# Expert routing: the lower weight parts of seven "up" chunks move from GpSimd to VectorE

## The chip, the cores and the metric

The kernel runs on one core of a Trainium2 chip. The metric is the device time of the whole program in microseconds (us), from launch to the last output. Engines are named as in the profile: PE (TensorE), DVE (VectorE), ACT (ScalarE), POOL (GpSimd), SP (SyncE, which here issues the weight loads).

## What is computed

Three transformer blocks on 256 tokens of width 1024. The change touches the end of the first block, a product-key expert layer ("PEER"), of which this is the reference, cut:

```python
q = (ht @ w_q).reshape(T, PEER_HEADS, PEER_QDIM)
s1 = einsum('thd,nd->thn', q[..., :128], sub_k1); s2 = einsum('thd,nd->thn', q[..., 128:], sub_k2)
v1, i1 = top_k(s1, 16); v2, i2 = top_k(s2, 16)
cand = v1[..., :, None] + v2[..., None, :]          # 16 x 16 candidates per head
vals, pos = top_k(cand, 16)                          # 16 of 128*128 experts, for each of 8 heads
experts = take_along_axis(cand_idx, pos); gates = softmax(vals)
a = einsum('cd,chkd->chk', x, expert_u[experts])     # "up"
w = gelu(a) * gates
out = einsum('chk,chkd->cd', w, expert_v[experts])   # "down"
```

## The kernel before

It does not gather. It multiplies all 256 tokens with all 16384 expert rows ("up", 64 chunks of 256 experts), applies gelu, and later multiplies with a dense matrix of gates that the routing builds from the selected indices.

**Split weights.** Each float32 weight chunk arrives by one SP-issued DMA into `raw` (three buffers). `stream` then makes two parts of it: ACT writes the upper part `wh` (L99, two halves of 128x1024), and L101 writes the lower part `wl = raw - wh` in two halves, on DVE, or on POOL where `pool` is true. `wh` and `wl` have three buffers each, so ACT can begin chunk c+3 only when PE has done chunk c; the load of chunk c+3 into `raw` is issued when both halves of `wl` of chunk c are made. PE needs three products for each block of 128 (L117 to L119): the first two read `wh`, the third reads `wl`. A chunk is two outputs of 24 matmuls each, half 0 and half 1. Each output lies in one of two PSUM buffers (tag `tq`) until ACT has applied gelu to it (`ga`, L1020).

**Routing.** While PE does the query projection and then the first "up" chunks, DVE does the top-16 searches and the selection, for the token tiles t0 and t1 in turn: the candidates (L923), eight searches by MAX8, FIND_INDEX8, MATCH_REPLACE8 (L891 to L895), the softmax of the gates (`g`, L934 to L939, whose Exp is on ACT at L935 between two table loads), some integer work on positions (L943 to L957), then for each of two index lists a one-hot product (`eq`, L962 to L971: 128x2048 in 16-bit), whose result `idx` PE transposes (L973). After t1 follow 32 groups that build gates as one-hot matrices (E, B, A: L996 to L1000; matmuls L1005).

**Order.** `weave` lets the routing go one step and takes one "up" chunk at steps 7 to 19, so chunks 0 to 12 lie beside the searches and selections of t0 and t1; then two chunks in five steps. A scheduler then sets the order of the instructions on each engine, each of which runs its own in order. It sets DVE's splits where it holds them to be due, and ACT's Exp and PE's transposes of `idx` in between the gelus and the matmuls.

**Names.** Chunks 3 to 6 have the lower parts `wl_3500`, `wl_3575`, `wl_3650`, `wl_3718`; chunks 7 and 8 `wl_3809` and `wl_3895`; chunks 9 to 11 `wl_3992`, `wl_4067`, `wl_4142`; chunk 12, which is on DVE in both kernels, `wl_4210`. The transposed indices are `idx_3567`, `idx_3642` for t0 and `idx_4059`, `idx_4134` for t1. In the profile all of these are `wl` and `idx`.

Of the kernel before, what the change touches and what calls it, by code (L numbers as in the profile page):

```python
# [857 lines left out]
class Peer:  # L858
# [153 lines left out]
    def up(self):  # L1012
        k, nc = self.k, self.k.nc
        for c in range(64):
            hl = k.stream(k.a["peer_u"][c], pool=c < 12)
            for i in range(2):
                ps = k.tp((128, S), tag="tq")
                k.linear_stat(hl, i, ps)
                g = self.pool.tile([128, S], F32, tag="ga", name="ga", bufs=self.AHEAD)
                nc.scalar.activation(g, ps, AF.Gelu_apprx_tanh)  # L1020
                self.ga[c * 2 + i] = g
            yield

    def down(self, up):
        k, nc, pool = self.k, self.k.nc, self.rp
        acc = [[k.acc(name=f"o{t}{h}") for h in range(2)] for t in range(2)]
# [14 lines left out]
        for c in range(64):  # L1041
            if c % 4 == 0:
                G = pool.tile([128, S // self.GRP, 8, self.GRP], F32, tag="g8", name="G", bufs=2)
                nc.scalar.dma_start(G, self.gd[:, :, c * 2:c * 2 + 8, :])
            for _ in range(1 if c else 5):
                next(up, None)
            vs = [x.rearrange("p (e h n) -> p e h n", e=2, h=2) for x in k.stream(k.a["peer_v"][c])]
            ws = []
            for i in range(2):
                e = c * 2 + i  # L1050
                w = self.ga.pop(e)
                w3 = w.rearrange("p (a b) -> p a b", b=self.GRP)
                nc.vector.tensor_tensor(w3, w3, G[:, :, e % 8, :], op=OP.mult)
                wh = pool.tile([128, S], F32R, tag="wth", name="wth", bufs=5)
                wl = pool.tile([128, S], F32R, tag="wtl", name="wtl", bufs=5)
                k.split(wh, wl, w)
                ws.append((wh, wl))
            if c < 62:
                for i in range(2):
                    part(c * 2 + i, vs, ws[i])  # L1060
            else:
                last += [(c * 2 + i, vs, ws[i]) for i in range(2)]
# [11 lines left out]
    def run(self):  # L1074
        up = self.up()
        done = [0]

        def n(i):
            x = i >= 7 if i < 20 else i % 5 in (0, 3)
            x = min(x, self.AHEAD // 2 - 5 - done[0])  # L1080
            done[0] += max(x, 0)
            return max(x, 0)
        with self.k.tc.tile_pool(name="route", bufs=1) as self.rp:
            weave(self.routing(), up, n)
        with ExitStack() as ctx:
            self.rp = ctx.enter_context(self.k.tc.tile_pool(name="down", bufs=1))
            self.k.work(ctx)
            self.down(up)
# [850 lines left out]
```

## Time and profile before

| | |
|---|---|
| median of 3 runs | 2859.41 us (2853.96 to 2859.89) |
| profiled execution | 2853.05 us, of it 2851.1 us span from first to last instruction |
| PE busy | 2744.9 us, 96% of the span |
| DVE busy | 1786.7 us, 63% |
| ACT busy | 1364.5 us, 48% |
| POOL busy | 294.8 us, 10% |

The stretch that the change touches lasts from about 343 us (chunk 3) to about 425 us (chunk 12). Shares over the whole span tell nothing of it; the windows and timelines of that stretch, in the section on rows, do. In a timeline a number in square brackets is the idle time of the engine just before the row, and the name behind it what ended that time.

### The profile page before, as it was taken

The numbers are of one execution on the slowest core, as the hardware profiler recorded it, in microseconds if no ns is written. First come the engines' busy times: TensorE is split into PE (matmuls) and PEld (weight loads), VectorE is DVE, ScalarE is ACT, GpSimd is POOL, SyncE is SP. The second block draws the span as 40 slices with busy tenths as digits, with TensorE's granted clock in tenths as the row PEclk, the third lists the DMA queues.
The fourth block names the chain that finished last, engine by engine and source line by source line (L and its number), as shares of the span: only waits on it lengthen the run. The fifth ranks groups of instructions, "written<-read, shape, count | busy, mean of one in ns | idle before, by whom it ended". The sixth has DMA issues, their size and how long they took to land.

```text
span 2851.1 us, 44585 instructions
## 1 busy us (share of the span) xinstructions
PE 2744.9 (96%) x18132; PEld 2481.8 (87%) x18132; DVE 1786.7 (63%) x3018; ACT 1364.5 (48%) x2302; POOL 294.8 (10%) x314
## 2 busy tenths in 40 slices
PE   7899979999999999999999999999999999999999
PEld 6787979989999888988899899897998878889897
DVE  6757698775555556547865555676645665466654
ACT  5544445544444555444544444524444454454543
POOL 2101650000000000003300000151001110000100
PEclk9989999999999999999999999999999999999999
DMA  5423436896565555554255455524554334433452
GB/s 207 152 97 134 150 121 254 288 321 219 204 215 205 192 192 198 201 190 167 87 188 190 165 209 189 196 89 148 193 192 142 134 116 156 161 133 121 161 192 104
DMA packets 105982, 496.74 MB, mean 174 GB/s; under 512 B 11040, under 2 KB 44320, under 8 KB 50224
## 3 DMA queue, kind: packets, MB, share of 16 engines
q1 hardware_dynamic: 61632, 443.15, 44.8%
q10 hardware_dynamic: 44144, 50.74, 5.4%
q8 instruction: 142, 2.33, 0.3%
q14 instruction: 64, 0.52, 0.1%
HBM read 476.03 MB, written 17.83 MB: 173 GB/s over the span
## 4 chain that ended last, share of the span: by engine, by line
PE 63%; issue 23%; DVE 7%; POOL 3%; ACT 3%; DMA 1%; POOLq 0%; ACTq 0%; DVEq 0%
PE acc L119 6%; PE acc L117 6%; PE acc L118 6%; PE tp L119 4%; PE tp L117 4%; PE tp L118 4%; PE o L1037 4%; PE o L1036 4%; PE o L1039 4%; PE o L316 2%; PE o L317 2%; PE o L319 2%; DVE wl L101 1%; PE o L1667 1%; PE o L1664 1%
## 5 line engine op out<-in xcount | busy, mean ns | idle before, releaser
L101 DVE TENSOR_TENSOR wl<-raw,wh 128x1024 fp32r<-128x1024 f32 x808 | 972.0, 1224 | 633.9 <-ACT wh L99 633.2
L99 ACT CAST wh<-raw 128x1024 fp32r<-128x1024 f32 x848 | 862.4, 1041 | 712.2 <-PE acc L118 234.9
L118 PE MATMUL acc<-xx,wh 128*128 128x256 f32 x1504 | 423.9, 282 | 0.0
L119 PE MATMUL acc<-xx,wl 128*128 128x256 f32 x1504 | 423.4, 281 | 0.0
L117 PE MATMUL acc<-xx,wh 128*128 128x256 f32 x1504 | 423.2, 281 | 0.0
L117 PE MATMUL tp<-xx,wh 128*128 128x256 f32 (+1 forms) x1440 | 410.7, 285 | 5.6 <-ACT ga L1020 5.6
L119 PE MATMUL tp<-xx,wl 128*128 128x256 f32 (+1 forms) x1440 | 409.0, 284 | 2.1 <-DVE wl L101 2.1
L118 PE MATMUL tp<-xx,wh 128*128 128x256 f32 (+1 forms) x1440 | 408.6, 284 | 0.0
L117 PEld LDWEIGHTS acc<-xx,wh 128*128 128x128 f32 x1504 | 284.9, 189 | 0.3 <-ACT xs L278 0.3
L119 PEld LDWEIGHTS acc<-xx,wl 128*128 128x128 f32 x1504 | 285.1, 190 | 0.0
L118 PEld LDWEIGHTS acc<-xx,wh 128*128 128x128 f32 x1504 | 283.0, 188 | 0.0
L117 PEld LDWEIGHTS tp<-xx,wh 128*128 128x128 f32 x1440 | 274.0, 190 | 9.1 <-ACT ga L1020 6.0
L118 PEld LDWEIGHTS tp<-xx,wh 128*128 128x128 f32 x1440 | 274.1, 190 | 2.5
L119 PEld LDWEIGHTS tp<-xx,wl 128*128 128x128 f32 x1440 | 273.5, 190 | 2.5 <-DVE wl L101 2.5
L117 PE MATMUL acc<-wh,xx 128*128 128x256 f32 (+2 forms) x672 | 228.3, 341 | 2.5 <-ACT xx L112 2.2
L118 PE MATMUL acc<-wl,xx 128*128 128x256 f32 (+2 forms) x672 | 223.5, 333 | 5.3 <-DVE wl L101 5.3
L147 POOL TENSOR_SCALAR va<-ss 128x1 f32<-128x1 f32 (+1 forms) x49 | 24.3, 496 | 1949.8 <-ACT junk L143 1768.1
L119 PE MATMUL acc<-wh,xx 128*128 128x256 f32 (+2 forms) x672 | 221.9, 333 | 2.1 <-DVE xx L113 2.1
L1037 PE MATMUL o<-wl,wth 128*128 128x512 f32 x512 | 200.2, 391 | 2.1 <-DVE wl L101 2.1
L1036 PE MATMUL o<-wh,wth 128*128 128x512 f32 x512 | 200.7, 392 | 0.0
L1039 PE MATMUL o<-wh,wtl 128*128 128x512 f32 x512 | 159.6, 390 | 0.0
L118 PEld LDWEIGHTS acc<-wl,xx 128*128 128x128 f32 x672 | 132.2, 197 | 16.7 <-DVE wl L101 6.9
(508 smaller groups left out, 4853.4 us busy)
## 6 DMA issues: line engine op xcount, KB each, us to landing
raw<-in_ffn_in_dram SPq DMA_DIRECT2D x88, 1024.0 KB, 4.9
raw<-in_peer_u_dram SPq DMA_DIRECT2D x64, 1024.0 KB, 5.0
raw<-in_peer_v_dram SPq DMA_DIRECT2D x64, 1024.0 KB, 4.9
raw<-in_ffn_out_dram SPq DMA_DIRECT2D x44, 1024.0 KB, 4.9
raw<-in_w_up_dram SPq DMA_DIRECT2D x32, 1024.0 KB, 4.9
raw<-in_w_down_dram SPq DMA_DIRECT2D x32, 1024.0 KB, 4.9
gd<-gt ACTq DMA_DIRECT2D x16, 1024.0 KB, 5.9
G<-gd ACTq DMA_DIRECT2D x16, 1024.0 KB, 7.0
```

The costliest lines, as they stand in the source:

```text
L99: nc.scalar.copy(h[:, c], r[:, c])
L101: eng.tensor_tensor(l[:, c], r[:, c], h[:, c].bitcast(F32), op=OP.subtract)
L117: mm(out, ah, bh, start=start, stop=False)
L118: mm(out, ah, bl, start=False, stop=False)
L119: mm(out, al, bh, start=False, stop=stop)
L316: mm(acc[t][h], hi[:, k, ts], wv[0][:, h], start=st, stop=False)
L317: mm(acc[t][h], hi[:, k, ts], wv[1][:, h], start=False, stop=False)
L319: mm(acc[t][h], lo[:, k, ts], wv[0][:, h], start=False, stop=sp)
L1036: mm(acc[t][h], wh, vh[:, h], start=st, stop=False)
L1037: mm(acc[t][h], wh, vl[:, h], start=False, stop=False)
L1039: mm(acc[t][h], wl, vh[:, h], start=False, stop=sp)
L1664: mm(acc[t][h], xh, wh[:, h], start=st, stop=False)
```

## The change

The lower parts of chunks 3 to 6 and 9 to 11 are made by DVE; those of 0, 1, 2, 7 and 8 stay on POOL, and from 12 on nothing is different.

```diff
         for c in range(64):
-            hl = k.stream(k.a["peer_u"][c], pool=c < 12)
+            hl = k.stream(k.a["peer_u"][c], pool=c in (0, 1, 2, 7, 8))
```

The scheduler orders the rows anew on DVE, ACT and PE; SP's order stays. On DVE, at the end of t0's searches (`mr`, `val`, `pos` are the search's, `g` is the gates' softmax):

```order
 L895 MAX_INDEX pos_3289<-val_3288,mr_3388 128x8
 L893 MATCH_REPLACE mr_3394<-val_3288,cand_3285 128x112
-L962 CAST ib_3559<-i1_2473 128x128
+L101 TENSOR_TENSOR wl_3500<-raw_3497,wh_3499 128x1024
 L894 MAX val_3288<-mr_3394 128x8
-L962 CAST ib_3634<-i2_2474 128x128
+L101 TENSOR_TENSOR wl_3500<-raw_3497,wh_3499 128x1024
 L895 MAX_INDEX pos_3289<-val_3288,mr_3394 128x8
 L934 TENSOR_TENSOR g_3462<-val_3288 128x128
```

Both halves of chunk 3's split stand behind all eight searches, and ahead of the last search's two final steps and of `g`.

On DVE, from t0's second one-hot product to the second `idx` and the candidates of t1 (`eq_3561` is the first product, `eq_3636` the second), the rows before:

```order
L967 TENSOR_TENSOR eq_3636<-eq_3636,ib_3634 128x2048
L969 TENSOR_TENSOR eq_3561<-eq_3561 128x512
L969 TENSOR_TENSOR eq_3636<-eq_3636 128x1024
L969 TENSOR_TENSOR eq_3561<-eq_3561 128x256
L969 TENSOR_TENSOR eq_3636<-eq_3636 128x512
L971 TENSOR_TENSOR idx_3567<-eq_3561 128x128
L969 TENSOR_TENSOR eq_3636<-eq_3636 128x256
L923 TENSOR_TENSOR cand_3777<-v1_2471,v2_2472 128x8x64
L971 TENSOR_TENSOR idx_3642<-eq_3636 128x128
```

and of the change:

```order
L971 TENSOR_TENSOR idx_3567<-eq_3561 128x128
L967 TENSOR_TENSOR eq_3636<-eq_3636,ib_3634 128x2048
L101 TENSOR_TENSOR wl_3650<-raw_3647,wh_3649 128x1024
L969 TENSOR_TENSOR eq_3636<-eq_3636 128x1024
L101 TENSOR_TENSOR wl_3650<-raw_3647,wh_3649 128x1024
L969 TENSOR_TENSOR eq_3636<-eq_3636 128x512
L101 TENSOR_TENSOR wl_3718<-raw_3715,wh_3717 128x1024
L969 TENSOR_TENSOR eq_3636<-eq_3636 128x256
L101 TENSOR_TENSOR wl_3718<-raw_3715,wh_3717 128x1024
L971 TENSOR_TENSOR idx_3642<-eq_3636 128x128
```

The first `idx` is no longer mixed with the second product, and the splits of chunks 5 and 6 stand between it and the second `idx`; chunk 4's split stands just ahead of these rows, inside the first product's tree (L969).

On ACT, the place of t1's Exp, before:

```order
L99 CAST wh_3894<-raw_3892 128x1024
L935 ACT_TABLE_LOAD
L935 ACTIVATE g_3954<-g_3954 128x128
L1020 ACT_TABLE_LOAD
L1020 ACTIVATE ga_3748<-tp_3723 128x256
```

and of the change:

```order
L1020 ACTIVATE ga_3839<-tp_3814 128x256
L935 ACT_TABLE_LOAD
L935 ACTIVATE g_3954<-g_3954 128x128
L1020 ACT_TABLE_LOAD
L1020 ACTIVATE ga_3866<-tp_3841 128x256
```

`ga_3748` is the gelu of chunk 6's half 0, `ga_3839` and `ga_3866` those of chunk 7's two halves: the Exp stands three gelus later. t0's Exp stays ahead of chunk 3's first gelu, with one cast more in front of it. On PE the first two matmuls of half 1 of chunks 4 and 5 move ahead of half 0's third, and the transpose of the first `idx` stands after 10 matmuls of chunk 4's half 1 instead of 16, that of the second after 17 of chunk 5's half 1 instead of ahead of chunk 5. In t1 ten rows of the one-hot groups (E, B, A, each 128x1024 in 16-bit) that lay ahead of the second `idx` on DVE come behind it, and the first half of chunk 12's split comes ahead of it.

## Rows read from the trace of the kernel before

**Rows 1.** The page, part 1: busy us, share of the span, instructions.

```profile
PE 2744.9 (96%) x18132; PEld 2481.8 (87%) x18132; DVE 1786.7 (63%) x3018; ACT 1364.5 (48%) x2302; POOL 294.8 (10%) x314
```

**Rows 2.** Windows: stretch, length, busy of each engine, granted clock, DMA share, GB/s.

```profile
361.90:378.50 16.60, 6.63 (x41) 6.35 (x41) 16.53 (x30) 5.25 (x8) 7.20 (x3) 0.80 0.37 127
...
392.90:417.30 24.40, 18.85 (x145) 18.59 (x145) 24.40 (x35) 11.14 (x17) 16.82 (x7) 0.93 0.39 131
```

**Rows 3.** Waits of PE, 340 to 424: waiter, releaser, us, times, longest.

```profile
PE tp L973 <- DVE idx L971: 10.1, 3, 7.3
PE tp L117 <- ACT ga L1020: 5.6, 2, 2.9
```

**Rows 4.** Timeline of PE: start, us, engine, line, op, [idle before, releaser].

```profile
356.40 0.28 PE L119 MATMUL tp<-xx,wl 128*128 128x256 f32 x1
356.52 0.28 PE L117 MATMUL tp<-xx,wh 128*128 128x256 f32 x1
...
364.70 0.39 PE L117 MATMUL tp<-xx,wh 128*128 128x256 f32 x1 [2.70 <-ACT ga L1020]
364.92 0.28 PE L118 MATMUL tp<-xx,wh 128*128 128x256 f32 x1
...
368.82 0.28 PE L117 MATMUL tp<-xx,wh 128*128 128x256 f32 x1
...
378.50 0.44 PE L973 MATMUL tp<-ident,idx 128*128 128x128 f32 x1 [7.28 <-DVE idx L971]
...
387.01 0.27 PE L977 MATMUL tp<-ident,g 128*128 128x128 f32 x1
...
395.87 0.58 PE L117 MATMUL tp<-xx,wh 128*128 128x256 f32 x1 [2.92 <-ACT ga L1020]
...
417.30 0.33 PE L973 MATMUL tp<-ident,idx 128*128 128x128 f32 x1 [2.63 <-DVE idx L971]
...
423.46 0.33 PE L973 MATMUL tp<-ident,idx 128*128 128x128 f32 x1 [0.16 <-DVE idx L971]
```

**Rows 5.** Timeline of POOL: chunk 8's split, then those of chunks 10 and 11.

```profile
388.26 4.78 POOL L101 TENSOR_TENSOR wl<-raw,wh 128x1024 fp32r<-128x1024 f32 x2 [1.85 <-ACT wh L99]
...
404.40 11.89 POOL L101 TENSOR_TENSOR wl<-raw,wh 128x1024 fp32r<-128x1024 f32 x4 [2.79 <-ACT wh L99]
```

**Rows 6.** Timeline of DVE, rows that lie beside a split on POOL.

```profile
349.14 2.21 DVE L923 TENSOR_TENSOR cand<-v,v 128x512 f32<-128x512 f32 x1
...
363.33 2.34 DVE L957 TENSOR_TENSOR xb<-x,y 128x128 f16<-128x128 f32 x1
...
388.16 0.26 DVE L893 MATCH_REPLACE8 mr<-val,cand 128x112 f32<-128x112 f32 x1
388.34 2.45 DVE L962 CAST ib<-i 128x128 f16<-128x128 uint32 x1
...
404.76 3.42 DVE L965 TENSOR_TENSOR eq<-xb,iota 128x2048 f16<-128x2048 f16 x1
```

**Rows 7.** Timeline of DVE, rows with POOL idle.

```profile
360.61 0.25 DVE L962 CAST ib<-i 128x128 f16<-128x128 uint32 x1
...
361.41 0.26 DVE L934 TENSOR_TENSOR g<-val 128x128 f32<-128x128 f32 x1
...
373.73 1.22 DVE L965 TENSOR_TENSOR eq<-xb,iota 128x2048 f16<-128x2048 f16 x1
374.86 0.69 DVE L969 TENSOR_TENSOR eq<-eq 128x1024 f16<-128x1024 f16 x1
...
423.33 4.62 DVE L101 TENSOR_TENSOR wl<-raw,wh 128x1024 fp32r<-128x1024 f32 x4
```

**Rows 8.** Timeline of ACT: t1's Exp.

```profile
393.82 0.31 ACT L935 ACTIVATE g<-g 128x128 f32<-128x128 f32 x1 [2.95 <-DVE g L934]
```

**Rows 9.** DMA issues, 330 to 440: queue, op, count, KB each, median us to landing.

```profile
raw<-in_peer_u_dram SPq DMA_DIRECT2D x14, 1024.0 KB, 4.9
```

**Rows 10.** Windows: the one-hot groups behind the change, columns as in rows 2.

```profile
440.00:540.00 100.00, 97.87 (x1033) 95.78 (x1032) 94.45 (x136) 58.96 (x103) 0.00 (x0) 0.98 0.72 262
```

## Prediction

> **What bounds the kernel now.** First the page: PE is busy for 96% of the span [rows 1], so a change elsewhere pays only where PE waits or runs slowly. The windows around chunks 3 to 12 show two such places: from 361.9 to 378.5 PE is busy for 6.6 of 16.6 us, from 392.9 to 417.3 for 18.9 of 24.4, while DVE has no gap in either [rows 2]. The waits of PE there have two releasers: `idx` on DVE (10.1 us) and a gelu on ACT (5.6 us) [rows 3]. The timeline of PE gives the places: 2.70 us at 364.70, 7.28 at 378.50, 2.92 at 395.87, 2.63 at 417.30, 0.16 at 423.46, in all 15.7 us [rows 4]. The waits for a gelu are DVE's too: ACT stood before the Exp, which waited 2.95 us for DVE's `g` [rows 8], and the gelu was queued behind it. So DVE bounds this stretch.
>
> After three of these waits PE also runs slowly: at 364.70 the next matmul starts 0.22 us later, against 0.12 at 356.40, and the granted clock of that window is 0.80 of the 2.4 GHz level, which is what a part at 1.2 GHz gives [rows 2, 4]. The slow spacing ends just before 368.82 [rows 4]: some 18 matmuls of 0.095 us too much, 1.7 us. Three times that is 5.1 us. **The loss before is 15.7 + 5.1 = 20.8 us.**
>
> **Why DVE is late.** Beside a split on POOL many DVE rows take 2.2 to 3.4 us. An L962 takes 2.45 beside POOL and 0.25 with POOL idle; an L965 3.42 and 1.22 [rows 6, 7]. Their ends fit the ends of POOL's halves (a split of two halves lasts 4.78 [rows 5]): each waits for one half, some 2.2 us. MATCH_REPLACE8 beside POOL takes 0.26: the searches don't wait [rows 6]. I count twelve such rows from 349 to 417, 26 us together; five are shown. When both engines have work queued they take turns: at 404.40 POOL's four halves stretch to 11.89 us, 2.97 each [rows 5].
>
> **The change, part by part.** *Removed from POOL:* seven splits. With them the twelve waits of DVE go, if nothing new collides (two of them lie beside chunk 8, which stays on POOL, but those rows now come ahead of it): -26 us on DVE. *Added to DVE:* 14 halves of 1.14 us (four in 4.62 [rows 7]): +16.0 us. *Moved:* ten one-hot rows go behind the second `idx` of t1, 0.6 each by the row of that size [rows 7], -6.1; chunk 12's split comes ahead of it, +2.3 or half of that. ACT and PE get no work added; SP's order is the same.
>
> The total doesn't say where PE waits, so I follow the new order with the durations of these rows.
>
> *Chunk 3.* Its split stands behind eight searches. DVE's row at 349.14 no longer waits, which brings all behind it forward by 1.6 us, so the split starts where L962 stood, 360.61 - 1.6 = 359.0 [rows 6, 7], and its first half is there at 360.2. PE starts this chunk at 356.52 and needs `wl` at the third matmul, 356.75 [rows 4]: **a new wait of 3.5 us**, and by the rows above a slow clock behind it, 1.7. Before, PE did not wait here. Queued behind the split on DVE are `g` and the Exp; `g` comes at 361.7 instead of 361.41 [rows 7], and the gelu that the Exp holds up isn't due until PE ends the half at 364.5, so this wait (2.70 before) is gone. PE ends chunk 3 at 367.4.
>
> *Chunk 4.* From `g` to the second product row DVE needs 5.8 us unhindered (1.9 to L957 [rows 6, 7], 1.4 for eight small rows, 2.5 for the large ones), to 367.5; the first half is there at 368.75, PE has waited 0.4 for a gelu and 0.5 for the split. `idx_3567` is there at 372.65, when PE gets to it: 0.15. **In all 1.1 us, where 7.28 was.**
>
> *Chunks 5 to 7.* DVE goes on with the second product and chunk 5's split, to 376.6; PE waits 0.25 for a gelu. But chunk 7 is still POOL's. Its load goes out when chunk 4's split is done, at 370.4, and takes 4.9 [rows 9]; ACT casts it from 375.5, so POOL starts at 376.5. DVE then has a tree row, chunk 6's two halves, another tree row and `idx_3642` queued, 3.2 us of work of the kind that waits. Taking turns, it waits for both halves of POOL, 4.6 us: `idx_3642` at 384.3 instead of 379.7. PE stands before it from 379.7: **4.7 us, and 1.7 of slow clock.** By this PE ends chunk 6's half 0 at 389.5; before it began at 387.01 [rows 4] and ended 2.8 later, at 389.9. Up to here all is spent again.
>
> On this the Trainium skill, SBUF — State Buffer, section "Who interferes with whom", says that a DVE instruction with two SBUF inputs contends with a GpSimd instruction that reads SBUF, that whichever issues first holds the port for its whole length, and that one with a single SBUF input outside the fast modes doesn't contend. The rows above agree (2.21 and 0.26 us); were DVE to issue first at 376.6, this rule would give the lighter collision, the first rival.
>
> *t1.* PE now needs 2.84 us for each half (24 times 0.118) from 389.5 on. Chunk 8 on POOL runs from 387.4 to 392.2 beside searches, which don't wait. Searches end at 394.6, then chunk 9's split, needed by PE at 403.8: no wait. `g` at 397.5, Exp, table load, gelu at 399.7; since the Exp stands three gelus later, PE doesn't need that buffer before 400.9. **The 2.92 goes, with its slow clock.** Nothing on POOL hinders the products: `idx_4059` at 409.3, PE there at 409.5; `idx_4134` at 414.1 to 414.2, PE there at 415.25. **The 2.63 goes.** The DVE account agrees: 423.3 (the end of that `idx` before, where the splits of [rows 7] begin) - 6.1 + 16.0 + 2.3 - 26 + 4.6 = 414.1.
>
> *Behind it.* From 440 to 540 DVE is busy for 94 of 100 us and PE for 98 [rows 10]. DVE enters it about 7 us earlier than before and PE 8; the 6 us in which DVE is not busy there cover the difference of 1, so I count it as nothing. Without that cover it costs that 1 us.
>
> **Sum.** Loss after: 3.5 + 1.7 + 1.1 + 0.25 + 4.7 + 1.7 = 13.0. Gain 20.8 - 13.0 = 7.8; the walk (415.35 against 423.5 at chunk 11) gives 8.2. I take 8. On the profiled execution, 2851.1 span and 2 around it, that is 2853.05 - 8 = 2845. The median of the three runs is 2859.41, 6.4 above it; taken from the median, which is what will be compared, 2851.4, rounded to **2851**. Bounds: a slow clock may or may not follow a wait (it did not after 2.63 us [rows 4]): 1.7 either way for each of the two, so 4.6 to 11.4 by the clock alone.
>
> **Rivals.**
> *A lighter collision at chunk 7.* If DVE gets through more rows first, or the load of chunk 7 lands later, one half of POOL is waited for, or none. For: the order of two queued engines hangs on tenths of a us. Against: ACT has the cast ready before DVE's queue is through. Price: 2.4 to 4.7 us and the slow clock of 1.7 saved, gain 10.5 to 14.5: 2845 to 2849. Chance 0.18.
>
> *t1 loses again.* The margins there are 0.1, 1.0 and 1.2 us. If two DVE rows of t0's gates (L981, L982) come 0.4 us later, they meet chunk 8's first half, and all of t1 is 2.4 us later; a wait of 1 to 3 us and a slow clock take 3 to 5 back: gain 3 to 5, 2855. Likewise if chunk 3's wait is longer by some us. With all that ends within 0.2% (5.7 us, what a measurement here can tell from no change): 0.24.
>
> *DVE's long rows are not POOL's doing, so the splits only add.* Then `idx_4134` comes at 423.3 - 6.1 + 16.0 + 2.3 = 435.5, 12 us later than before, and PE with it: 2871. It decides from the point where less than 12 of the 26 us are relieved. Against it speak the short rows with POOL idle [rows 7]; for it only that a wait for a port isn't itself a row. Chance 0.06.
>
> That the change does nothing is excluded: the order shows the 14 rows on DVE.
>
> **How the numbers follow.** Forecast (gain 5.7 to 10.5) 0.52, lighter collision 0.18, within 0.2% 0.24, slower 0.06. Faster by over 0.2%: 0.52 + 0.18 = 0.70. The range: from 2842 (10 to 11 us below the profiled execution, since an execution may lie there rather than at the median) to 2858 (a gain of 1.5 from the median).
>
> **What would show it.** Right: one wait of PE for `wl` near 356.8 of about 3.5 us; one for `idx` near 379.7 of about 4.7, beside chunk 7 on POOL; none of over 1 us between 390 and 425; L953, L954, L965 and L967 at their short lengths except beside chunks 7 and 8; `idx_4134` near 414. Wrong: a PE wait for chunk 4, 5, 9 or 10's `wl` of several us, DVE rows still long with POOL idle, or the later one-hot stage growing by what was gained.

## The result, and the profile after

The changed kernel takes 2839.82 us (median of 9 runs, 2833.34 to 2848.18), the kernel before beside it 2857.15 (9 runs): ratio 0.9945, 95% interval 0.9931 to 0.9960. It is faster, by more than forecast (2851), and the time lies below the range (2842 to 2858).

The profiled execution took 2846.34 us, span 2844.6. Page, part 1, of the kernel after:

```profile
PE 2746.9 (97%) x18132; PEld 2483.8 (87%) x18132; DVE 1781.1 (63%) x3032; ACT 1364.4 (48%) x2302; POOL 261.8 (9%) x300
```

VectorE has 14 rows more than in [rows 1] and yet is busy 5.6 us less; GpSimd gave up 33. The waits of TensorE, 340 to 424, that answer to [rows 3]:

```profile
PE tp L119 <- DVE wl L101: 4.1, 2, 3.8
PE tp L117 <- ACT ga L1020: 3.5, 3, 3.0
```

No wait for `idx` is left, where there were 10.1 us. The places, in TensorE's timeline, answer to [rows 4]:

```profile
356.26 0.39 PE L119 MATMUL tp<-xx,wl 128*128 128x256 f32 x1 [3.81 <-DVE wl L101]
...
363.98 0.39 PE L117 MATMUL tp<-xx,wh 128*128 128x256 f32 x1 [0.24 <-ACT ga L1020]
...
388.25 0.58 PE L117 MATMUL tp<-xx,wh 128*128 128x256 f32 x1 [3.00 <-ACT ga L1020]
```

The first is chunk 3's new wait for its split; the last is a wait for a gelu ahead of chunk 7's half 1, where none was forecast (its path is shown under "Which chunks on GpSimd still cost"). The first L910 stands at 295.8 here and at 299.8 in the trace before, so times of the prediction are to be read 4.0 us earlier. Windows after, columns as in [rows 2]:

```profile
343.04:361.90 18.86, 15.05 (x114) 14.84 (x113) 18.86 (x107) 8.60 (x13) 0.00 (x0) 0.91 0.17 58
361.90:378.50 16.60, 15.81 (x130) 15.15 (x129) 16.50 (x26) 7.53 (x14) 5.87 (x1) 1.00 0.38 128
378.50:392.90 14.40, 11.40 (x84) 11.19 (x83) 14.40 (x73) 5.77 (x10) 7.67 (x4) 0.88 0.58 221
392.90:417.30 24.40, 24.40 (x209) 24.40 (x209) 24.40 (x45) 13.47 (x23) 0.00 (x0) 1.00 0.51 183
```

From 361.9 to 378.5 TensorE is now busy for 15.81 of 16.60 us, where it was 6.63. Two stretches with a lowered clock are left (0.91, 0.88), each about a wait; there were three, two of them in [rows 2] (0.80, 0.93) and one between:

```profile
378.50:392.90 14.40, 14.39 (x107) 14.25 (x107) 14.40 (x69) 6.80 (x11) 9.40 (x4) 0.87 0.22 75
```

**A measure with less scatter.** The medians carry the scatter of the whole program: the changed kernel's runs alone lie 15 us apart. I therefore measure in each trace the stretch from the start of the first score matmul (L910, queries times keys) to the start of the last one-hot matmul (L1005). It is 299.8 to 544.1 = 244.3 us before and 295.8 to 529.1 = 233.3 after; copies of both give 244.3 and 233.0 (below). It has two parts. Up to the first L1005 it is 135.2 us before and 125.6 after, in the copies 135.2 and 125.5: **there the change is worth 9.6 to 9.7 us.** The rest, the one-hot groups, takes 109.1 and 107.7 us. This 1.4 is a slow clock of TensorE, which stands behind the same wait before and not after. The wait and the window from it to the end of the groups, before and then after:

```profile
535.28 0.38 PE L119 MATMUL tp<-xx,wl 128*128 128x256 f32 x1 [2.08 <-DVE wl L101]
535.28:544.30 9.02, 9.02 (x85) 8.79 (x86) 3.51 (x4) 4.09 (x7) 0.00 (x0) 0.81 0.65 242
...
521.72 0.39 PE L119 MATMUL tp<-xx,wl 128*128 128x256 f32 x1 [2.08 <-DVE wl L101]
521.72:529.30 7.58, 7.58 (x86) 7.40 (x87) 3.52 (x4) 3.99 (x7) 0.00 (x0) 1.00 0.73 276
```

The copies agree with this, but of the two traces of another kernel (chunks 0 to 2 alone on GpSimd, below) one has this slow clock and one hasn't (109.0 and 107.6). So the whole stretch gains 11.0 to 11.3 us, and whether the 1.4 in it belongs to the change is open.

### The profile page after: what moved, and what is told of

Same layout as the page of the kernel before. It is cut to its first block, busy times and chain, and to the rows that moved or that the text cites. A ratio compares the mean times of both kernels' runs of the same rounds, so it can differ in the third digit from the quotient of the medians.

```text
span 2844.6 us, 44587 instructions
## 1 busy us (share of the span) xinstructions
PE 2746.9 (97%) x18132; PEld 2483.8 (87%) x18132; DVE 1781.1 (63%) x3032; ACT 1364.4 (48%) x2302; POOL 261.8 (9%) x300
## 4 chain that ended last, share of the span: by engine, by line
PE 63%; issue 23%; DVE 6%; POOL 3%; ACT 3%; DMA 3%; ACTq 0%; POOLq 0%; DVEq 0%; SPq 0%
PE acc L119 6%; PE acc L117 6%; PE acc L118 6%; PE tp L119 4%; PE tp L117 4%; PE tp L118 4%; PE o L1037 4%; PE o L1036 4%; PE o L1039 4%; PE o L316 2%; PE o L317 2%; PE o L319 2%; DVE wl L101 2%; PE o L1667 1%; PE o L1665 1%
## 5 line engine op out<-in xcount | busy, mean ns | idle before, releaser
L101 DVE TENSOR_TENSOR wl<-raw,wh 128x1024 fp32r<-128x1024 f32 x822 | 989.0, 1223 | 630.1 <-ACT wh L99 629.7
```

The costliest lines, as they stand in the source:

```text
L101: eng.tensor_tensor(l[:, c], r[:, c], h[:, c].bitcast(F32), op=OP.subtract)
```

## The experiments

All kernels edit the one line of the change, unless another diff stands here. "Loss" is wait and slow clock of TensorE.

### Both kernels again

The changed kernel:

> The changed kernel once more, for a second trace and more times. The two traces at hand differ by 9.7 us from the first of the query-projection transposes of the scores (L910) to the last transpose of idx (L973), by 1.4 more up to the end of the one-hot groups, and by 6.5 over the span, while the medians differ by 17. Theory 'local and clock': the stretch from chunk 3 to the one-hot groups is again 9 to 11 us shorter than before, and what is beyond that comes and goes elsewhere with the granted clock: executions with a mean clock of 0.985 lie some 8 us below those of 0.982. Rival 'all local': the stretch itself is some 16 us shorter in this trace, and the first trace was an exception. Time: 2836 to 2846 by both.

2841.67 us (6 runs) against 2854.82 before (29 runs on that chip); ratio 0.9950 (0.9931 to 0.9969); stretch 233.0. The large waits are the same two, the second 2.51.

The kernel before, written as an edit of the changed one:

```diff
-            hl = k.stream(k.a["peer_u"][c], pool=c in (0, 1, 2, 7, 8))
+            hl = k.stream(k.a["peer_u"][c], pool=c < 12)
```

> The kernel before once more, for a second trace. 'Local and clock': the same five waits of PE between 340 and 424 (15.7 us together, within 1 us), total 2854 to 2860; any difference of the span from the first trace shows in the granted clock of other stretches. 'All local': the waits of PE in this stretch differ by 5 us or more from the first trace. Ratio to before 0.999 to 1.001.

2854.60 us, ratio 0.9995 (0.9982 to 1.0009); stretch 244.3. So in these two kernels the stretch repeats; what lies ahead of it (294.4 to 301.2 us in all traces, whatever the edit) does not.

### One half of the change alone

Only chunks 3 to 6 to VectorE:

```diff
+            hl = k.stream(k.a["peer_u"][c], pool=c < 3 or 6 < c < 12)
```

> Only the first half of the change: chunks 3 to 6 on VectorE, 9 to 11 on GpSimd as before. If DVE's long rows come from POOL's splits beside them, the rows of t0 (L957, L953, L965 near 363 to 371) are short and the wait of 7.3 us for the first idx is gone, against a new wait of 3.5 to 4 for chunk 3's lower part; t1 keeps its long rows and its waits (2.9 and 2.6). Gain 4 to 8 us. If the gain of the change sat in t1 alone, 0 to 2.

2856.61 us, ratio 0.9997 (0.9982 to 1.0011); stretch 244.4, up to the first L1005 135.7: a gain of nothing, where 4 to 8 was expected. TensorE's waits, 340 to 424, and two of their places:

```profile
PE tp L117 <- ACT ga L1020: 6.2, 4, 3.0
PE tp L119 <- DVE wl L101: 4.1, 2, 3.8
PE tp L973 <- DVE idx L971: 4.0, 1, 4.0
```

```profile
399.69 0.58 PE L117 MATMUL tp<-xx,wh 128*128 128x256 f32 x1 [2.96 <-ACT ga L1020]
...
416.70 0.47 PE L973 MATMUL tp<-ident,idx 128*128 128x128 f32 x1 [4.05 <-DVE idx L971]
```

The wait of 7.28 is gone, but t1's first `idx` wait has grown from 2.63 to 4.05, and beside the gelu wait that was there (now 2.96) stands a new one, of 2.75 at 392.09. TensorE is there 116.9 us after the first L910; before it was 117.5. What t0 gained, TensorE waits for in t1, where VectorE is as late as ever.

Only chunks 9 to 11 to VectorE:

```diff
+            hl = k.stream(k.a["peer_u"][c], pool=c < 9)
```

> Only the second half: chunks 9 to 11 on VectorE, 3 to 6 on GpSimd as before. The waits of t0 stay (2.7, 7.3). The wait of 2.6 for idx in t1 goes, with long rows L965, L967, L969 near 400 to 416; the wait of 2.9 for a gelu behind the Exp goes only if it was DVE's chunk 8 collision that is left (in the changed kernel 3.0 us were left there). Gain 2 to 6 us; the gains of the two halves add up to that of the whole within 3 us if each part acts in its own stretch.

2854.01 us, ratio 0.9994 (0.9980 to 1.0008); stretch 240.8, up to the first L1005 131.8, a gain of 3.4. TensorE's waits, 340 to 424:

```profile
PE tp L973 <- DVE idx L971: 7.3, 1, 7.3
PE tp L117 <- ACT ga L1020: 5.4, 2, 2.7
```

Nothing and 3.4 are not 9.6. The halves don't add up; the waits that are left say why. Each half frees one of the two engines: t0's part lets TensorE come early to t1, t1's part lets VectorE be ready for it. Only together does the gain pass through.

### Who makes VectorE's rows long

A kernel with nothing but four GpSimd subtractions of 128x1024 beside eight VectorE rows:

> The disputed cost by itself; the kernel leaves the whole computation out and only copies x to the output. POOL makes four subtractions of 128x1024 (two SBUF inputs) while DVE has eight instructions queued: (a) eight subtractions that don't depend on each other, (b) eight that each wait for the one before, (c) eight MAX8; then (a) and (b) beside four POOL memsets, which read nothing. Theory 'held': DVE keeps the port as long as it has an instruction ready; in (a) its rows start every 1.14 us and POOL's first row lasts about 9 + 2.4 us; in (b) the wait between two instructions lets POOL in, and DVE rows take 3.4 us or more until POOL is through. Rival 'turns': in (a) as in (b) the two engines alternate and DVE's rows take 3.4 us. MAX8 is not hindered by either. Beside memsets DVE's rows keep 1.2 us in (a) and (b).

Timeline: start, us, engine, line, op, [idle before]. In order: GpSimd alone, VectorE alone, both, VectorE's MAX8 beside GpSimd, GpSimd's memsets beside VectorE.

```profile
8.28 9.23 POOL L1917 TENSOR_TENSOR po<-raw,go 128x1024 f32<-128x1024 f32 x4 [7.84 <-ACT go L1931]
18.62 9.17 DVE L1924 TENSOR_TENSOR dv<-raw,go 128x1024 f32<-128x1024 f32 x8 [18.62 <-ACT go L1931]
...
40.16 17.74 DVE L1924 TENSOR_TENSOR dv<-raw,go 128x1024 f32<-128x1024 f32 x8 [1.17 <-ACT go L1931]
40.27 13.15 POOL L1917 TENSOR_TENSOR po<-raw,go 128x1024 f32<-128x1024 f32 x4 [22.77 <-ACT go L1931]
...
78.40 10.06 DVE L1928 MAX8 mx<-go 128x8 f32<-128x1024 f32 x8 [1.19 <-ACT go L1931]
78.44 9.26 POOL L1917 TENSOR_TENSOR po<-raw,go 128x1024 f32<-128x1024 f32 x4 [6.09 <-ACT go L1931]
87.64 7.19 POOL L1919 MEMSET po<- 128x1024 f32 x8
89.65 9.17 DVE L1924 TENSOR_TENSOR dv<-raw,go 128x1024 f32<-128x1024 f32 x8 [1.19 <-ACT go L1931]
```

Beside each other VectorE's eight take 17.74 us instead of 9.17 and GpSimd's four 13.15 instead of 9.23: they take turns, each of GpSimd's rows lasting 3.3 us. Of the two theories on record, "turns" holds. MAX8 costs GpSimd nothing (9.26), and memsets cost VectorE nothing (9.17). (The memsets planned beside the chain ran earlier, so that section says nothing.)

In the kernel itself, with before's placing, GpSimd writes zeros twice instead of subtracting for chunks 3 to 11; their lower parts are thus left out:

```diff
-                eng.tensor_tensor(l[:, c], r[:, c], h[:, c].bitcast(F32), op=OP.subtract)
+                if pool == 2:
+                    eng.memset(l[:, c].bitcast(F32), 0.0)
+                    eng.memset(l[:, c].bitcast(F32), 0.0)
+                else:
+                    eng.tensor_tensor(l[:, c], r[:, c], h[:, c].bitcast(F32), op=OP.subtract)
...
+            hl = k.stream(k.a["peer_u"][c], pool=c < 12 and (2 if c > 2 else 1))
```

> The kernel before, but for chunks 3 to 11 POOL writes zeros twice in place of the subtraction (the lower parts of these chunks are left out of the result), so POOL is busy at the same places and reads no SBUF. Stretch from the first L910 to the last L1005: 244.3 us in both traces of before, 233.2 in both of the changed kernel. If DVE's long rows come from POOL's reads, they are short here without any work moved to DVE: the waits for idx and for the gelu behind the Exp go, stretch 224 to 230. Rival, DVE is late for another reason (its own queue, POOL being slow): 240 to 245.

One run, 2840.74 us; stretch 226.9, 17.4 less than before, up to the first L1005 119.4, 15.8 less. GpSimd still works in the same places, though for less time (1.9 us a half instead of 2.39). TensorE's waits, 340 to 424, and a row of VectorE beside GpSimd's memsets (lines are 4 further down, so L969 is L965):

```profile
PE tp L121 <- ACT ga L1024: 2.7, 2, 1.7
PE tp L977 <- DVE idx L975: 0.9, 1, 0.9
```

```profile
358.28 1.92 POOL L102 MEMSET wl<- 128x1024 f32 x2 [2.04 <-PE tp L123]
...
359.04 1.22 DVE L969 TENSOR_TENSOR eq<-xb,iota 128x2048 f16<-128x2048 f16 x1
```

So it is GpSimd's reading, not its being busy, that makes VectorE late. The Trainium skill, SBUF — State Buffer, section "Who interferes with whom", says this of VectorE instructions with two SBUF inputs: a GpSimd instruction that reads SBUF contends with them, one that only writes doesn't. The small program agrees (17.74 us beside subtractions, 9.17 beside memsets), and so does the kernel (an L965 3.42 us beside subtractions [rows 6], 1.22 here).

### Which chunks on GpSimd still cost

Chunk 3 back on GpSimd, to save its new wait:

```diff
+            hl = k.stream(k.a["peer_u"][c], pool=c in (0, 1, 2, 3, 7, 8))
```

> The changed kernel with chunk 3 back on POOL. The wait of 3.8 us for chunk 3's lower part and its slow clock go; POOL's chunk 3 lies beside the candidates row L923 (2.2 instead of 0.7 us) and otherwise beside searches, which it doesn't hinder. Stretch from the first L910 to the last L1005 227 to 231 us (233.2 in the changed kernel), about 2836 in all. If the wait only moves on to chunk 4, whose split then stands in the selection, 232 to 236.

2845.89 us (10 runs), ratio 0.9969 (0.9955 to 0.9983); stretch 236.9, where 227 to 236 was expected; up to the first L1005 127.8, which is 2.2 worse than the change. The wait of 3.8 is gone, but a gelu wait of 2.7 and one of 0.9 for `idx` stand there instead; the gelu wait of 3.00 stays (2.9).

Chunks 7 and 8 off GpSimd too:

```diff
+            hl = k.stream(k.a["peer_u"][c], pool=c < 3)
```

> Chunks 7 and 8 on DVE as well. The collision that delays the gates' rows (L981, L982: 1.9 and 2.2 us in the changed kernel) goes, DVE gets 4.6 us more. If the 2.5 to 3.0 us wait for the gelu behind t1's Exp comes from that collision, it goes and the stretch is 229 to 233 us; if DVE's queue is the bound in t1, splits come late and the stretch is 234 to 240.

One run, 2838.04 us; stretch 232.5. TensorE's waits, 340 to 424:

```profile
PE tp L119 <- DVE wl L101: 4.6, 3, 3.8
PE tp L117 <- ACT ga L1020: 1.1, 3, 0.7
PE tp L973 <- DVE idx L971: 0.5, 1, 0.5
```

The gelu wait of 3.00 is gone, so it came from chunks 7 and 8 on GpSimd. Its path stands in the changed kernel's trace. In order: GpSimd's second half of chunk 7; SP's load of chunk 9; ACT's cast of chunk 9, the gelu behind it, and t1's Exp.

```profile
379.04 2.39 POOL L101 TENSOR_TENSOR wl<-raw,wh 128x1024 fp32r<-128x1024 f32 x1
381.46 0.33 SPq L108 DMA_DIRECT2D raw<-in_peer_u_dram  x1
386.87 1.05 ACT L99 CAST wh<-raw 128x1024 fp32r<-128x1024 f32 x1 [6.88 <-DMA raw<-in_peer_u_dram]
387.83 0.38 ACT L1020 ACTIVATE ga<-tp 128x256 f32<-128x256 f32 x1
...
392.31 0.31 ACT L935 ACTIVATE g<-g 128x128 f32<-128x128 f32 x1 [1.58 <-DVE g L934]
```

The load of chunk 9 goes out when chunk 7's lower part is done, at 381.43; chunk 6's had been done at 375.34. So it doesn't follow chunk c by c+3 here, as it does in the kernel before; why, no run shows. ACT stands before the cast for 6.88 us, and the gelu behind it, which TensorE needs from 385.25, is done at 388.2. The Exp comes only then and holds TensorE up nowhere. With chunks 7 and 8 on VectorE the same load goes out at 374.05, just after chunk 6's lower part. Run six times:

> GpSimd keeps chunks 0 to 2 alone, chunks 7 and 8 go to VectorE too; timed in rounds. Both theories agree on the local gain: its stretch from the first gather of the routing to the last product behind it was 232.5 us in one look, 0.8 less than the changed kernel's 233.3 and 11.8 less than before's 244.3, so the median should lie 10 to 14 us under the kernel before on the same chip, ratio 0.995 to 0.9965, and 0 to 2 us under the changed kernel. If the pair 7 and 8 on GpSimd were worth something elsewhere, it would be 2 us or more over the changed kernel.

2843.51 us (6 runs), ratio 0.9956 (0.9939 to 0.9973); stretch 231.0. Up to the first L1005 the two traces give 123.5 and 123.4 us, 2.0 to 2.2 better than the change; the one-hot groups differ by the slow clock told of above. By the medians no difference can be told.

### Why the collision at chunk 7 did not come

In the changed kernel GpSimd's first half of chunk 7 begins at 372.63, and VectorE's rows up to the second `idx` and beyond run at their own length. GpSimd's row, then VectorE's, same timeline columns:

```profile
372.63 6.45 POOL L101 TENSOR_TENSOR wl<-raw,wh 128x1024 fp32r<-128x1024 f32 x1 [33.66 <-ACT wh L99]
```

```profile
372.80 1.21 DVE L101 TENSOR_TENSOR wl<-raw,wh 128x1024 fp32r<-128x1024 f32 x1
373.93 0.28 DVE L969 TENSOR_TENSOR eq<-eq 128x256 f16<-128x256 f16 x1
374.13 1.21 DVE L101 TENSOR_TENSOR wl<-raw,wh 128x1024 fp32r<-128x1024 f32 x1
375.27 0.28 DVE L971 TENSOR_TENSOR idx<-eq 128x128 f32<-128x128 f16 x1
...
377.27 1.88 DVE L981 CAST gT<-res 128x128 f16<-128x128 f32 x1
...
379.34 2.23 DVE L982 TENSOR_TENSOR gT<-res,gT 128x128 f16<-128x128 f32 x1
```

GpSimd was held off 4.1 us (6.45 less its own 2.39), VectorE not at all until 377. With chunk 3 on GpSimd too it was held off longer still: its row at 374.39 lasted 9.14 us. In the kernel before, at 404.40, they took turns [rows 5, 6]. Why? First guess: the kinds of rows in VectorE's list.

> Only two GpSimd subtractions of 128x1024 a section beside a forced order of VectorE rows, everything else of the kernel is left out; one scalar copy sets both engines off at once. Sections: (1) five VectorE subtractions into float32, (2) five into the matmul type, (3) a subtraction, three fp16 additions of 128x1024, a subtraction, (4) fp16 additions of 128x512 between subtractions into float32, (5) the same between subtractions into the matmul type. Theory 'always turns': in all five each engine's rows alternate while GpSimd has work, its two take 3.2 to 3.4 us each behind the first (6 to 7.5 us in all), and no section lets VectorE run two rows at their own 1.2 us. Theory 'mixed shapes hold GpSimd off': in sections 4 and 5 (or 2 and 5, if the type does it) VectorE's rows run at 1.2 and about 0.6 us one behind the other, and the first GpSimd row takes 5 to 8 us, until VectorE's list is through; sections 1 and 3 alternate.

Turns in all five sections. From the fourth:

```profile
43.36 3.38 POOL L1935 TENSOR_TENSOR po<-raw,go 128x1024 fp32r<-128x1024 f32 x1 [3.52 <-ACT go L1933]
44.45 2.56 DVE L1930 TENSOR_TENSOR eq<-eq,eq 128x512 f16<-128x512 f16 x1
```

An addition that takes 0.41 us alone lasts 2.56. So the kinds of rows alone don't decide. Second guess: it matters that GpSimd comes when VectorE is already running.

> Everything of the kernel is left out but two GpSimd subtractions of 128x1024 a section, each set off by a scalar copy of its own, so that the first comes in the middle of a VectorE list that has already begun to run back to back (in the micro kernels before, both engines began together). Sixteen sections: four lists (fp16 additions of 128x512 between subtractions into the matmul type; subtractions alone; fp16 additions of 128x1024 alone; the first list with a scalar-written operand of its own for each subtraction), each at four different delays of GpSimd's start. Theory 'always turns': GpSimd's first row ends at most one VectorE row (0.4 to 1.3 us) later than its own 2.3 us, and VectorE's next row is held to 2.5 to 3.4 us, in all sixteen. Theory 'who is running keeps it': GpSimd's first row takes 4 us or more, until VectorE's list is through or comes to a gap, in all sixteen, and no VectorE row is lengthened ahead of that. Theory 'the list decides': the sections of one or two of the four lists (the mixed ones) hold GpSimd off at every delay, the others take turns. If it goes with the delay and not with the list, the phase at which GpSimd arrives in a VectorE row decides.

This one miscarried: GpSimd ran ahead of the sections and met VectorE in the first five only, in turns. The scalar copies were then tied to VectorE's first row:

> Everything of the kernel is left out but a VectorE list and two GpSimd subtractions of 128x1024 a section. A scalar copy of VectorE's first row sets GpSimd off, so its first row comes while VectorE's list is running back to back. Twelve sections: three lists (fp16 additions of 128x512 among subtractions; the same with a scalar-written operand of its own for each subtraction, so that each has a semaphore to look at; fp16 additions of 128x1024), with GpSimd idle for 5 to 15 us before or for over 35 us (30 more VectorE subtractions ahead), at two delays. In the kernel GpSimd was held off (4.1 and 6.8 us) where it came after more than 20 us without work into a list with such subtractions, and not where it had worked 3 us before. Theory 'idle': held off (first row 4 us or more, VectorE's rows at their own 1.2 and 0.4 us) in the six sections with the long idle stretch, in no other. Theory 'operand of its own': held off in the four sections of the second list, in no other. Theory 'always turns': in none; then what held it off in the kernel stays open.

GpSimd was held off in seven places (its row 8.99 to 9.35 us long, to the end of VectorE's list), among them all six with a long idle stretch; but one of the seven had none, only 13.7 us of idleness. Where it had been idle for less, turns. That spoke for idleness, with a border to be found:

> Everything of the kernel is left out but a VectorE list (fp16 additions of 128x512 and subtractions of 128x1024) and one GpSimd subtraction of 128x1024 a section that comes into the middle of it. Ten sections with GpSimd idle for about 10, 11, 12, 13, 15, 17, 20, 25, 10 and 25 us before. Theory 'idle': turns (GpSimd's row under 3.5 us) in the short ones, held off until VectorE's list ends (8 us or more) in the long ones, with one border between 11.0 and 13.7 us. Four more sections of about 25 us, in which GpSimd does something small (128x64) some 5 us before it comes: a memset, a subtraction, a memset, a subtraction. If its own idleness decides, all four take turns; if the last time that it read operands does, the two with a subtraction take turns and the two with a memset are held off; if VectorE's undisturbed run decides, all four are held off.

GpSimd's timeline, the sections with 3, 4 and 6 more VectorE subtractions ahead; then one in which it does a memset, and one in which it does a small subtraction, on the way:

```profile
59.92 2.45 POOL L1947 TENSOR_TENSOR po<-raw,pg 128x1024 fp32r<-128x1024 f32 x1 [13.79 <-ACT pg L1946]
77.29 9.35 POOL L1947 TENSOR_TENSOR po<-raw,pg 128x1024 fp32r<-128x1024 f32 x1 [14.92 <-ACT pg L1946]
95.75 9.36 POOL L1947 TENSOR_TENSOR po<-raw,pg 128x1024 fp32r<-128x1024 f32 x1 [9.10 <-ACT pg L1946]
...
199.57 0.15 POOL L1942 MEMSET mark<- 128x64 f32 x1 [10.36 <-DVE mark L1940]
205.26 9.35 POOL L1947 TENSOR_TENSOR po<-raw,pg 128x1024 fp32r<-128x1024 f32 x1 [5.54 <-ACT pg L1946]
224.99 13.00 POOL L1944 TENSOR_TENSOR mark<-mark,raw 128x64 f32<-128x64 f32 x1 [10.38 <-DVE mark L1940]
```

The idleness theory falls: after 13.79 us GpSimd got its turn, after 9.10 it was held off, and a memset 5.5 us before changed nothing. What orders the ten plain sections is how long VectorE had run without a gap when GpSimd came: 2.4, 3.4, 3.6, 4.7 and 5.9 us, turns; 7.0 and more, held off to the end of its list. Even the small subtraction of 128x64 lasted 13.00 us, 11.5 us into such a run. Of the outcomes on record for the four sections with something small on the way, the third came: all were held off. The same was asked of the kernel itself, with small GpSimd subtractions in chunks 3 to 6 of the changed kernel:

```diff
+            if touch:
+                nc.gpsimd.tensor_tensor(self.touch, r[:, c][:, :64], h[:, c][:, :64].bitcast(F32), op=OP.subtract)
...
+            hl = k.stream(k.a["peer_u"][c], pool=c in (0, 1, 2, 7, 8), touch=2 < c < 7)
```

> The changed kernel, and GpSimd does a small extra subtraction (128x64, into a tile that nobody reads) at each half of chunks 3 to 6, so that it has worked a few us before chunk 7 reaches it. Theory 'a GpSimd that has just worked gets its turns': chunk 7's halves and VectorE's rows alternate (GpSimd's first row under 3.5 us where it was 6.45, VectorE's rows of 1.22 at 2.5 to 3.4), the indices come later, TensorE waits 3 to 6 us for idx_3642 before its gather, and the stretch from the first gather to the last product behind it is 236 to 240 us instead of 233.3: the collision at chunk 7 that the prediction priced at 4.7 us with 1.7 of slow clock. Theory 'the place in VectorE's list decides': GpSimd's first row stays at 6 us or more, no wait for the index, the stretch 233 to 235.

One run, 2845.76 us; stretch 234.5. GpSimd's timeline, the last two small ones (chunk 6's) and then chunks 7 and 8:

```profile
365.20 12.41 POOL L104 TENSOR_TENSOR touch<-raw,wh 128x64 fp32r<-128x64 f32 x2 [10.09 <-ACT wh L100]
377.57 9.49 POOL L102 TENSOR_TENSOR wl<-raw,wh 128x1024 fp32r<-128x1024 f32 x4
```

The first of these two lasted 12.0 us, where the six small ones before took 0.32 each, until VectorE's list came to its searches at 376.95. It came after 10.09 us of idleness, where 13.79 us were no hindrance in the small program, so idleness is out here too. No wait for `idx` came, and up to the first L1005 it is 125.6 us, as in the change.

What fits most of it is VectorE's run: how long it had done these rows (subtractions, 16-bit rows, small casts and the like) with no gap, no search and no hold-up between, when GpSimd came. In the stretch of the kernels, counted from the rows: held off after 15.0 us (changed kernel, chunk 7), 15.0 (chunks 3 to 6 alone), 10.9 (chunk 3 on GpSimd) and 7.3 (the small subtractions); turns after 1.6, 3.5 and 1.7 us (kernel before, at 363.03, 396.83 and 404.40). The border was put together after the runs and no run was made to test it, and one of the sections with an operand of its own was held off after 4.3 us, where others took turns after 4.7 and 5.9. The border and the mechanism stay open; shown is that GpSimd's idleness doesn't decide it, nor the kinds of rows alone.

## Why the prediction was wrong, point by point

**Bound and loss before: right.** 20.8 us of waits and slow clock on TensorE, by VectorE; without GpSimd's reading the stretch is 17.4 us shorter (15.8 up to the first L1005), though VectorE then has fewer rows than after the change.

**Chunk 3: right.** 3.5 us said, 3.81 measured, until 356.26 (360.2 said, less the 4.0), with the slow clock behind it (window 0.91).

**Chunks 4 and 5: right, a little large.** 1.1 and 0.25 said; 0.24 and 0.31 for chunk 4, 0.24 for 5.

**Chunk 7: the step that failed.** "Taking turns, it waits for both halves of POOL" put 4.7 us of wait and 1.7 of slow clock before `idx_3642`; 0 came. The place was right (GpSimd came at 372.63; said was 376.5, less the 4.0), what happens there was not. `idx_3642` stood ready at 375.55, with every row ahead of it at its own length. Taking turns was read from one place, 404.40, 1.7 us after VectorE had itself been held up, and carried to a place where it had run freely for 15.0 us. The rival "a lighter collision" named the outcome, but gave it to tenths of a us, and the chance with it; the runs show that it comes each time.

**t1: the second failed step.** The forecast had no wait of over 1 us here; 3.00 (2.51 in the copy) and a window at 0.88 stand there. It isn't the Exp: "The 2.92 goes, with its slow clock" held, since the Exp comes at 392.31 and no wait of TensorE follows from it. The step that failed is the walk of t1. It has chunk 8's and chunk 9's splits and the Exp, but puts at nothing the way from GpSimd's chunk 7 over the load of chunk 9 and ACT's cast to the gelu (rows above, 379.04 to 387.83). Both failed steps have one cause: what spared `idx_3642` held back chunk 7's lower part, and with it this load. Without the 4.1 us for which GpSimd was held off, the gelu would have been done by about 384.1, before TensorE needed it at 385.25 (an estimate, with the rest unchanged). Had the forecast collision come, TensorE would have been there at 395.2 - 4.0 = 391.2, late enough for the gelu.

The rival "t1 loses again" had the price, 3 to 5 (3.00 and 1.7), but by luck. Its L981 and L982 did meet GpSimd (1.88 and 2.23 us, rows above, at 377.27 and 379.34; 2.24 and 0.27 in the kernel before), but the wait has another cause. The 2.63 for `idx` did go.

**Behind it: as said, but for the clock.** The one-hot groups took 107.7 us instead of 109.1, by the slow clock of 535.28 that may or may not come.

The sum with the measured terms: loss after = 3.81 + 1.7 + 0.55 + 0.24 + 3.00 + 1.7 = 11.0 (the windows give both 1.7 again: 18.86 times 0.09, 14.40 times 0.12). So 20.8 - 11.0 = 9.8 against 9.6 measured up to the first L1005, where 7.8 was forecast. The two failed steps are worth 6.4 one way and 4.7 the other. That the gain came out so near to the forecast is luck.

**The medians: the larger part of the miss.** From 2851.4 to 2839.82 are 11.6 us. 2.3 of them are the base: the forecast was taken from 2859.41, the median of three runs, and beside the changed kernel it was 2857.15 (later 2854.82, 2854.67 and 2856.13). 3.2 are the stretch, 11.2 with the groups where 8 was said. 6.1 lie outside the stretch; in the second comparison, where 13.2 us were gained, it is 2.0. From the profiled execution, 2853.05 - 11.2 gives 2841.9, and 2853.05 - 8 would have been 2845.

What lies outside looks like scatter of the clock. Ahead of the stretch nothing depends on the edit. Behind it the changed kernel's profiled execution takes 8.5 us more than before's (2315.5 against 2307.0), and TensorE is at 1.2 GHz for 67.0 us there against 52.3; half the difference is 7.4. Its copy takes 2.8 us less than before's copy (2308.7 against 2311.5). Among the first nine runs of the changed kernel a granted clock of 0.979 goes with 2847.69 us and 0.986 with 2833.34. Why one execution has more slow clock than another, and whether the change has a part in it, stays open.

**"DVE's long rows are not POOL's doing": refuted** by the kernel with the zeros and by the small program. That the change would be faster by over 0.2% held.

## What to carry to other kernels

Where two engines hinder each other's reads, moving work from the idle one to the busy one can make the busy one faster: 14 rows of 1.2 us were added to VectorE and its busy time fell by 5.6. When two stages feed each other in turn, test the halves of a change together as well as alone: here they were worth nothing and 3.4 us, and 9.6 together. When a step of the forecast makes an engine come earlier or later, walk on from there with all queues: here the next thing that TensorE met was a gelu behind a late load. Take a wait back to the first cause that the trace shows: the wait here looked like the Exp's and was a DMA's. For a small gain, measure a stretch between two landmarks of the trace: up to the first L1005 three kernels repeated to 0.1 us where the medians scattered by several. Do not hang a forecast on the median of three runs.

## What the hardware showed that was not expected

- Two engines that hinder each other don't always take turns. When both begin together, VectorE's 1.2 us rows last 3.35 and GpSimd's 2.3 us rows 3.3. When GpSimd came into a VectorE run of subtractions and 16-bit rows of 7 us or more without a gap, it waited to the run's end, its row 9.35 and 13.00 us long, and VectorE was not slowed meanwhile. Among other rows it isn't so: at 1347.74 in the kernel before, GpSimd came after 25.2 us without a gap, into rows of L1189, and neither its row (2.40) nor theirs (0.48) were slowed.
- Length doesn't protect a row: an addition of 0.41 us lasted 2.56 in turns, a GpSimd subtraction of 128x64 lasted 13.00.
